# A two-layer decoder trunk on one core: the gating layer norm's scale and shift folded into the mixing's bias step, the rotation of queries and keys on VectorE alone, odd values in two slots

## The chip, the cores and the metric

The kernel runs on 1 core of one Trainium2 chip. The metric is device time in microseconds (us) of one execution. Three runs of the kernel before gave 1886.30, 1886.41 and 1890.41 us; the median is 1886.41.

## The reference

The input is x, 1 x 512 x 1024 in float32. Two layers are computed, each as x + 1/2 SwiGLU(RMSNorm(x)), then x + Mixer(RMSNorm(x)), then x + 1/2 SwiGLU(RMSNorm(x)), with a hidden width of 2816; a last RMSNorm follows. The change touches the two mixers. Cut to what it touches:

```python
def layer_norm(x, g, b):
    mu = mean(x); var = mean((x - mu) ** 2)
    return (x - mu) * rsqrt(var + NORM_EPS) * g + b

def chunked_spatial_gating(z, ln_g, ln_b, w_s, b_s):      # even layer, z = gelu(h @ w)
    u, v = z[..., :512], z[..., 512:]
    v = layer_norm(v as (4 chunks of 128 tokens, 8 groups, 64 channels), ln_g, ln_b)
    w = lower triangle of w_s                             # (8 groups, 128, 128)
    mixed = einsum('gts,nsgd->ntgd', w, v) + b_s          # one bias per group and t
    return u * mixed

def apply_partial_rope(x, cos, sin):                      # on every q and k
    x1, x2, rest = x[..., :8], x[..., 8:16], x[..., 16:]
    return concat([x1 * cos - x2 * sin, x1 * sin + x2 * cos, rest])

def diff_attention(q, k, v, lam, subln_g, lambda_init):   # odd layer, 8 heads, two q/k maps each
    p = softmax(causal(q k^T / 8))                        # for either map
    o = (p[0] - lam * p[1]) @ v                           # v: 128 wide
    return rms_norm(o, subln_g) * (1 - lambda_init)
```

The even mixer concatenates 8 heads of causal attention with the gating's output; both mixers end with an output projection.

## The kernel before, in words

**Arithmetic.** x lies transposed, as 8 tiles of 128 channels x 512 tokens. Every product is made of three matmuls on halves: a float32 matrix is split into a rounded upper half (a copy on ScalarE, called ACT) and the rest (a subtraction on VectorE, called DVE), and `mm3` (L167 to L170) sums hi x hi, hi x lo and lo x hi in PSUM. So each chunk of weights of 128 x 1024 elements costs a copy (L120) and a subtraction (L121), whichever stage it is for. The tiles of the stream are `w_raw`, `w_hi` and `w_lo`.

**Order.** The work of all stages is one list of slots, `Stream` (L69 to L151). A slot has one or two chunks of weights and a function that issues its matmuls. In the mixers `run` (L125 to L140) first issues the splits of this slot's chunks and of the next slot's, then `step`, then the slot's matmuls. `st.later(n, fn)` puts `fn` into the step n slots on, and `st.mids` into the next one. So attention is woven between projections: what a head needs is issued some slots after its queries and keys, ahead of that slot's matmuls. Each engine works its own queue in order; a scheduler fixes that order when the program is built, near the order of the code, and lets some instructions whose inputs come sooner pass others. The chunks come by DMA over the queue of SyncE (SP).

**Even mixer (L782 to L936).** Slots: four chunks for the gate's second half v (`eg`, bank `pv`), four for its first half u (`eu`, bank `pu`), four for the attention's values (`ev`, `pv`), eight for queries and keys of four pairs of heads (`eqk`, `pq`), then the output projection (`eo`). The gate goes through Gelu on ACT into tiles `gv`. `center` (L825) subtracts the group means (`ln_m`) and sums squares (`ln_s`), one slot on for two token tiles and two slots on for the others. `finish_gate` (L836), three slots on, takes the reciprocal root (L191 to L202), multiplies by it on DVE (L840), by the scale on GpSimd (called POOL, L842) and adds the shift on POOL (L843); one slot later `split_gate` (L846) makes the halves `gh` (ACT, L333) and `gl` (DVE, L334). `mix_group` (L866), one for each pair of groups, in the second to fifth slot of `ev` and `eqk`, multiplies by the triangular weights `wsh`, `wsl`, adds the bias `bs` out of PSUM (L880), multiplies by u and splits. Scale and shift are two arrays of 128 x 512 (the same in every partition), loaded at the mixer's begin.

**Queries and keys.** `rotated` (L632) takes a projection out of PSUM. A shuffle on DVE swaps the channels of a pair into `sw` (L638), `q = pq * cos` is on DVE (L639), `sw = sw * sin` (L640) and `q = q + sw` (L641) are on POOL. In the next step the queries or keys are split: ACT copies (L653, keys L661) and DVE subtractions (L654, L662). This runs 24 times: 8 in the even mixer, 16 in the odd one.

**Attention.** For a head, `scores` gives four score products into banks `s`, the masked rows with their maxima (L688, DVE, tiles `e`), and exponentials (ACT, L690). `transposed` turns them through PE (`pt`) and splits them into `ph` (ACT, L711) and `pl` (DVE, L715); the last quarter, `pw`, isn't split. `attend` multiplies with the values into bank `o`. In the even mixer POOL scales the rows (L912), and the result is split by ACT and by DVE (L924, tile `ml`). The steps come EV = (3, 5, 6) slots after the keys. In the odd mixer DVE and POOL combine the two maps (L974 POOL, L976 DVE), and the result is normed over its 128 channels; the steps come OD = (3, 4, 6, 7, 9, 10) slots on.

**Odd mixer (L939 to L1045).** For each pair of heads there are five slots: queries, keys, queries, keys, and one slot of values (`values`, L1011) with two chunks. It makes 96 matmuls of 256 columns: for each of four token tiles eight k-tiles, three matmuls each.

**Room.** There are 8 banks of PSUM, one tag for all; tiles `w_raw`, `w_hi`, `w_lo` share 14 buffers, `e` has 3 and small temporaries have 7.

## Time and profile before

| What | Value |
| --- | --- |
| Median of three runs | 1886.41 us (1886.30 to 1890.41) |
| The profiled execution | 1890.68 us, of which the span from its first to its last instruction is 1888.9 us |
| Mean granted clock of TensorE | 0.986 |
| Busy share of the span | PE 97%, weight loads 88%, DVE 72%, ACT 46%, POOL 22% |
| HBM read and written | 237.40 MB and 2.10 MB, 127 GB/s over the span |
| Even mixer, odd mixer | about 366 to 566 us and 1270 to 1512 us of the span |

PE is TensorE, SP is SyncE. Times in the rows are microseconds unless marked ns. A matmul's duration includes its passage through a pipeline, so matmuls that follow each other overlap, and the distance of two starts is what each of them costs. "Busy" of an engine leaves out the time in which it waits. The granted clock is a share of 2.4 GHz.

### The profile page before, as it was taken

How to read it: one execution, taken by the hardware profiler on the slowest of the kernel's cores; microseconds unless marked ns; L12 is line 12 of the kernel's file. 1: busy time of each engine (PE TensorE's matmuls, PEld its weight loads, DVE VectorE, ACT ScalarE, POOL GpSimd, SP SyncE). 2: the span in 40 equal slices, each digit the busy share in tenths (PEclk: the TensorE clock that was granted, in tenths of full speed). 3: DMA queues.
4: the chain of work that ended last, by engine and by line, in shares of the span. 5: the costliest groups of instructions: out<-in, count | busy, mean ns of one | idle time of the engine just before them, and what ended most of it. 6: DMA issues, size and time to landing. Idle time of an engine off the chain costs nothing.

```text
span 1888.9 us, 29622 instructions
## 1 busy us (share of the span) xinstructions
PE 1834.6 (97%) x11612; PEld 1663.2 (88%) x11612; DVE 1359.1 (72%) x1949; ACT 875.4 (46%) x1302; POOL 415.0 (22%) x369
## 2 busy tenths in 40 slices
PE   7999999999898999999999999999899989999997
PEld 6989989878787989989899998988788779899896
DVE  8857748766758857748976685787798788578484
ACT  6524525433655524525554352544555455345252
POOL 1111011542522111010310111143433221110113
PEclk8999999999998999999999999999999999999999
DMA  7656656422334656656565565542232346566561
GB/s 201 176 141 154 168 122 168 129 66 69 90 97 94 177 141 152 168 124 156 134 152 154 129 178 135 149 135 67 90 90 90 95 95 169 144 157 163 124 160 45
DMA packets 197468, 247.74 MB, mean 131 GB/s; under 512 B 14272, under 2 KB 166480, under 8 KB 197328
## 3 DMA queue, kind: packets, MB, share of 16 engines
q1 hardware_dynamic: 153200, 202.81, 34.6%
q0 software_dynamic: 43552, 41.98, 15.1%
q8 instruction: 91, 1.49, 0.3%
q10 hardware_dynamic: 576, 1.05, 0.1%
q14 instruction: 49, 0.40, 0.1%
HBM read 237.40 MB, written 2.10 MB: 127 GB/s over the span
## 4 chain that ended last, share of the span: by engine, by line
PE 82%; DVE 7%; POOL 4%; ACT 3%; issue 2%; DMA 1%; SPq 0%; DVEq 0%; POOLq 0%; ACTq 0%
PE py L168 10%; PE py L170 10%; PE py L169 9%; PE pA L424 8%; PE pA L425 8%; PE pA L426 8%; PE pD L426 4%; PE pD L425 4%; PE pD L424 4%; PE pB L426 2%; PE pB L425 2%; PE pB L424 2%; POOL q L641 1%; DVE w_lo L121 1%; ACT e L690 1%
## 5 line engine op out<-in xcount | busy, mean ns | idle before, releaser
L120 ACT ACTIVATE w_hi<-w_raw 128x1024 fp32r<-128x1024 f32 (+1 forms) x450 | 467.8, 1042 | 619.7 <-PE py L169 210.9
L121 DVE TENSOR_TENSOR w_lo<-w_raw,w_hi 128x1024 fp32r<-128x1024 f32 (+1 forms) x450 | 558.5, 1242 | 178.6 <-ACT w_hi L120 144.3
L369 POOL DMA_DIRECT2D w_raw<-in_gu x160 | 173.6, 1209 | 985.2 <-DMA w_raw<-in_gu 522.4
L169 PE MATMUL py<-hl,w_hi 128*128 128x512 f32 x704 | 274.2, 389 | 0.0
L170 PE MATMUL py<-hh,w_lo 128*128 128x512 f32 x704 | 273.9, 389 | 0.0
L168 PE MATMUL py<-hh,w_hi 128*128 128x512 f32 x704 | 273.2, 390 | 0.0
L503 DVE SCALAR_TENSOR_TENSOR x<-py,x 128x512 f32<-128x512 f32 x96 | 66.0, 688 | 170.1 <-PE py L170 170.1
L424 PE MATMUL pA<-xh,w_hi 128*128 128x256 f32 x640 | 182.7, 285 | 0.0
L425 PE MATMUL pA<-xl,w_hi 128*128 128x256 f32 x640 | 182.1, 285 | 0.0
L426 PE MATMUL pA<-xh,w_lo 128*128 128x256 f32 x640 | 182.1, 285 | 0.0
L424 PE MATMUL pA<-xt,w_hi 128*128 128x256 f32 x640 | 181.2, 283 | 0.0
L426 PE MATMUL pA<-xt,w_lo 128*128 128x256 f32 x640 | 181.1, 283 | 0.0
L425 PE MATMUL pA<-xt,w_hi 128*128 128x256 f32 x640 | 181.1, 283 | 0.0
L169 PEld LDWEIGHTS py<-hl,w_hi 128*128 128x128 f32 x704 | 132.2, 188 | 27.6 <-DVE hl L482 0.8
L170 PEld LDWEIGHTS py<-hh,w_lo 128*128 128x128 f32 x704 | 132.2, 188 | 27.5
L168 PEld LDWEIGHTS py<-hh,w_hi 128*128 128x128 f32 x704 | 131.9, 188 | 27.8 <-ACT hh L477 1.2
L424 PEld LDWEIGHTS pA<-xh,w_hi 128*128 128x128 f32 x640 | 123.9, 194 | 1.5 <-ACT v L436 1.4
L425 PEld LDWEIGHTS pA<-xl,w_hi 128*128 128x128 f32 x640 | 123.9, 194 | 0.1
L426 PEld LDWEIGHTS pA<-xh,w_lo 128*128 128x128 f32 x640 | 123.9, 194 | 0.0
L424 PEld LDWEIGHTS pA<-xt,w_hi 128*128 128x128 f32 x640 | 122.9, 192 | 0.2 <-ACT v L436 0.2
L426 PEld LDWEIGHTS pA<-xt,w_lo 128*128 128x128 f32 x640 | 122.9, 192 | 0.0
L425 PEld LDWEIGHTS pA<-xt,w_hi 128*128 128x128 f32 x640 | 122.9, 192 | 0.0
(241 smaller groups left out, 4344.5 us busy)
## 6 DMA issues: line engine op xcount, KB each, us to landing
w_raw<-in_gu SPq DMA_DIRECT2D x402, 256.0 KB, 4.0
w_raw<-in_gu POOLq DMA_DIRECT2D x160, 256.0 KB, 5.3
w_raw<-in_wd SPq DMA_DIRECT2D x128, 256.0 KB, 3.0
w_raw<-in_wd SPq DMA_DIRECT2D x64, 192.0 KB, 2.5
w_raw<-in_oqk SPq DMA_DIRECT2D x16, 512.0 KB, 4.0
w_raw<-in_gu SPq DMA_DIRECT2D x14, 512.0 KB, 4.0
ks<-ks SPq DMA_DIRECT2D x24, 256.0 KB, 3.2
w_raw<-in_eqk SPq DMA_DIRECT2D x8, 512.0 KB, 3.7
```

The costliest lines, as they stand in the source:

```text
L120: nc.scalar.activation(hi, raw, AF.Copy)
L121: nc.vector.tensor_sub(lo, raw, hi.bitcast(F32))
L168: nc.tensor.matmul(o, sh, mh, start=first, stop=False)
L169: nc.tensor.matmul(o, sh, ml, start=False, stop=False)
L170: nc.tensor.matmul(o, sl, mh, start=False, stop=last)
L369: nc.gpsimd.dma_start(dst, src, accum_op=OP.add)
L424: nc.tensor.matmul(o, w[0][:, s], t[0], start=new and p + g == 0, stop=False, **go)
L425: nc.tensor.matmul(o, w[0][:, s], t[1], start=False, stop=False, **go)
L426: nc.tensor.matmul(o, w[1][:, s], t[0], start=False, stop=p == 3, **go)
L503: nc.vector.scalar_tensor_tensor(x[d], py[d], 0.5, x[d], op0=OP.mult, op1=OP.add)
L641: nc.gpsimd.tensor_add(q, q, sw)
L690: nc.scalar.activation(e, e, AF.Exp, bias=nm[:, i:i + 1], scale=-1.0, accum_out=su[:, o + i:o + i + 1])
```

## The change

Three parts:

- **Layer norm.** Scale and shift leave the gate: with G the normed gate, W (scale x G + shift) + bias is scale x (W G) + (shift x row sums of W + bias). The two are constant along the tokens that the mixing sums over, one of each for a channel, and after the mixing a channel is a partition. `biases`, four slots on, sums the rows of W by four matmuls with a tile of ones (banks `prow`) and adds shift x sums to `bs` in eight small operations. `mix_group` uses a multiply-add out of PSUM in place of an add. The POOL operations on `g` are gone, the halves of the gate are issued in `finish_gate`, and the scale and shift are loaded as two columns of four.
- **Rotation.** L640 and L641 are on DVE.
- **Odd values.** One slot with two chunks becomes two slots with one chunk each, both summing into the same two banks; the second one evacuates them. A pair of heads has six slots.

`warm` takes a tile of the temporaries in place of one of its own.

```diff
--- before.py
+++ after.py
@@ -169,7 +169,7 @@
         nc.tensor.matmul(o, sh, ml, start=False, stop=False)
         nc.tensor.matmul(o, sl, mh, start=False, stop=last)
 
-    warm = const.tile([P, 1], F32, name="warm")
+    warm = tmp("warm")[:, :1]
     nc.vector.memset(warm, 0.0)
     nc.scalar.activation(warm, warm, AF.Silu)
 
@@ -637,8 +637,8 @@
         sw, q = tmp("sw"), tmp("q")
         nc.vector.stream_shuffle(sw, pq, SWAP)
         nc.vector.tensor_mul(q, pq, cr)
-        nc.gpsimd.tensor_mul(sw, sw, sr)
-        nc.gpsimd.tensor_add(q, q, sw)
+        nc.vector.tensor_mul(sw, sw, sr)
+        nc.vector.tensor_add(q, q, sw)
         st.mids.append(lambda: place(q))
 
     class Pair:
@@ -801,13 +801,27 @@
                 hi, lo = split(ws, "ws", "r2")
                 wsh.append(hi)
                 wsl.append(lo)
-            ln = act.tile([P, 2, T], F32, name="ln", tag="e", bufs=EB)
-            for n, name in enumerate(("lng", "lnb")):
-                box[name] = ln[:, n]
-                nc.sync.dma_start(box[name], a["ln"][n])
+            ln = sm.tile([P, 2, 4], F32, name="ln", bufs=1)
+            for n in range(2):
+                nc.sync.dma_start(ln[:, n], a["ln"][n, 0:1].rearrange("o (m p) -> p (o m)", p=P))
+            box["ln"] = ln
             bs = act.tile([P, T], F32, name="bs", tag="e", bufs=EB)
             nc.sync.dma_start(bs, a["bs"])
-            box["bs"] = bs.rearrange("p (m t) -> p m t", t=P)
+            box["bs"] = bs = bs.rearrange("p (m t) -> p m t", t=P)
+            one = t2k("r2", "ones", F32R)[:, :P]
+            nc.vector.tensor_copy(one, ones1.to_broadcast([P, P]))
+
+            def biases():
+
+                for c in range(2):
+                    b = bank("prow")
+                    nc.tensor.matmul(b, one, wsh[c], start=True, stop=False)
+                    nc.tensor.matmul(b, one, wsl[c], start=False, stop=True)
+                    for i in range(4):
+                        m, r = 2 * c + i // 2, slice(i % 2 * 64, i % 2 * 64 + 64)
+                        nc.vector.scalar_tensor_tensor(bs[r, m], b[r, i * P:(i + 1) * P], ln[r, 1, m:m + 1],
+                                                       bs[r, m], op0=OP.mult, op1=OP.add)
+            st.later(4, biases)
 
         def by_group(g):
             return g.rearrange("p (g d) -> p g d", d=64)
@@ -839,9 +853,7 @@
                 g = cen[t]
                 nc.vector.tensor_tensor(by_group(g), by_group(g),
                                         rs[:, t, :, None].to_broadcast([P, 8, 64]), op=OP.mult)
-                nc.gpsimd.tensor_mul(g, g, box["lng"])
-                nc.gpsimd.tensor_add(g, g, box["lnb"])
-            st.later(1, lambda: [split_gate(t) for t in range(TT)])
+                split_gate(t)
 
         def split_gate(t):
             gh[t], gl[t] = split(cen[t], "g", "h")
@@ -877,8 +889,10 @@
                 bv = b.rearrange("p (n g t) -> p n g t", n=2, g=2)
                 for h in range(2):
                     r = slice(h * 64, h * 64 + 64)
-                    nc.vector.tensor_tensor(mixv[r, 2 * nn:2 * nn + 2], bv[r, :, h],
-                                            box["bs"][r, m:m + 1, :].to_broadcast([64, 2, P]), op=OP.add)
+                    nc.vector.scalar_tensor_tensor(mixv[r, 2 * nn:2 * nn + 2], bv[r, :, h],
+                                                   box["ln"][r, 0, m:m + 1],
+                                                   box["bs"][r, m:m + 1, :].to_broadcast([64, 2, P]),
+                                                   op0=OP.mult, op1=OP.add)
             nc.vector.tensor_mul(mix, mix, u[m])
             if m < 2:
                 mh[4 + m], ml[4 + m] = split(mix, "m", "h")
@@ -1009,15 +1023,27 @@
                 st.later(n, fn)
 
         def values(p):
-            def fn(wa, wb):
-                b = [bank("pv"), bank("pv")]
-                for t in range(TT):
-                    r = slice(t * P, (t + 1) * P)
-                    for k in range(KT):
-                        w = (wa, wb)[k // 4]
-                        s = slice((k % 4) * 256, (k % 4 + 1) * 256)
-                        mm3(b[t // 2][:, (t % 2) * 256:(t % 2 + 1) * 256], norm.hi[k][:, r], norm.lo[k][:, r],
-                            w[0][:, s], w[1][:, s], k == 0, k == KT - 1)
+            b = []
+
+            def half(n):
+                def fn(w):
+                    if n == 0:
+                        b.extend(bank("pv") for _ in range(2))
+                    for t in range(TT):
+                        r = slice(t * P, (t + 1) * P)
+                        o = b[t // 2][:, (t % 2) * 256:(t % 2 + 1) * 256]
+                        for k in range(4 * n, 4 * n + 4):
+                            s = slice((k % 4) * 256, (k % 4 + 1) * 256)
+                            go = {"skip_group_check": True}
+                            nc.tensor.matmul(o, norm.hi[k][:, r], w[0][:, s], start=k == 0 and t % 2 == 0,
+                                             stop=False, **go)
+                            nc.tensor.matmul(o, norm.hi[k][:, r], w[1][:, s], start=False, stop=False, **go)
+                            nc.tensor.matmul(o, norm.lo[k][:, r], w[0][:, s], start=False, stop=k == KT - 1, **go)
+                    if n == 1:
+                        evac()
+                return fn
+
+            def evac():
                 halves = [t2k("h", "v", F32R).rearrange("p (n c) -> p n c", n=2) for _ in range(3)]
                 vh = [halves[t][:, 0] for t in range(TT - 1)]
                 vl = [halves[t][:, 1] for t in range(TT - 1)]
@@ -1025,7 +1051,8 @@
                 for t in range(TT):
                     evac_value(t, b[t // 2][:, (t % 2) * 256:(t % 2 + 1) * 256], norm.col[:, t:t + 1], vh, vl, vw)
                 box["v", p] = (vh, vl, vw)
-            st.add([chunk(a["ov"][p, 0]), chunk(a["ov"][p, 1])], fn)
+            for n in range(2):
+                st.add([chunk(a["ov"][p, n])], half(n))
 
         for h in range(8):
             pair = Pair()
```

Lines after the edits have other numbers in the changed kernel: L840 is L854 there, L858 is L870, L880 is L892, L910 is L924, L924 is L938, L976 is L990.

**DVE, gate of the even mixer.** The rows are the stretch from the product with the reciprocal root to the first weights' splits after it (`gv` the gate, `gl` its lower halves, `u` the gate's other half, `w_lo` the weights). Before:

```order
L840 TENSOR_TENSOR gv<-gv,ln_rs 128x512 x4
L858 TENSOR_TENSOR u<-pu,R 128x512
L334 TENSOR_TENSOR gl<-gv,gh 128x512
L121 TENSOR_TENSOR w_lo<-w_raw,w_hi 128x1024
L334 TENSOR_TENSOR gl<-gv,gh 128x512 x3
L121 TENSOR_TENSOR w_lo<-w_raw,w_hi 128x1024
L858 TENSOR_TENSOR u<-pu,R 128x512
```

In the changed kernel, in the same place:

```order
L854 TENSOR_TENSOR gv<-gv,ln_rs 128x512 x3
L334 TENSOR_TENSOR gl<-gv,gh 128x512
L854 TENSOR_TENSOR gv<-gv,ln_rs 128x512
L334 TENSOR_TENSOR gl<-gv,gh 128x512
L870 TENSOR_TENSOR u<-pu,R 128x512
L334 TENSOR_TENSOR gl<-gv,gh 128x512
L121 TENSOR_TENSOR w_lo<-w_raw,w_hi 128x1024
L334 TENSOR_TENSOR gl<-gv,gh 128x512
L870 TENSOR_TENSOR u<-pu,R 128x512
L121 TENSOR_TENSOR w_lo<-w_raw,w_hi 128x1024 x5
```

The first weights' split stands behind three gate halves where it stood behind one. In the changed kernel DVE also has these rows ahead of the means of the gate (`bs` the bias, `prow` the row sums):

```order
L202 SCALAR_TENSOR_TENSOR rcol<-rs_3760,rs_3759 128x4
L842 TENSOR_REDUCE ln_m<-gv 128x8
L822 SCALAR_TENSOR_TENSOR bs<-prow,ln,bs 64x128 x7
L121 TENSOR_TENSOR w_lo<-w_raw,w_hi 128x1024
L822 SCALAR_TENSOR_TENSOR bs<-prow,ln,bs 64x128
L843 TENSOR_SCALAR ln_m<-ln_m 128x8
L842 TENSOR_REDUCE ln_m<-gv 128x8
L844 TENSOR_TENSOR gv<-gv,ln_m 128x512
```

Eight operations on `bs` stand at this place, between the first `ln_m` and the following ones; before there were none.

**DVE, attention of the even mixer.** The rows are around the third result of a head (`ml`, which frees its bank) and the probabilities after it (`pl`). Before:

```order
L662 TENSOR_TENSOR ks<-q,ks 64x512 x2
L121 TENSOR_TENSOR w_lo<-w_raw,w_hi 128x1024
L910 RECIPROCAL su<-su 128x4
L121 TENSOR_TENSOR w_lo<-w_raw,w_hi 128x1024
L924 TENSOR_TENSOR ml<-o,mh 64x512
L715 TENSOR_TENSOR pl<-pt,ph 128x512
L715 TENSOR_TENSOR pl<-pt,ph 128x384
```

In the changed kernel:

```order
L662 TENSOR_TENSOR ks<-q,ks 64x512 x2
L924 RECIPROCAL su<-su 128x4
L121 TENSOR_TENSOR w_lo<-w_raw,w_hi 128x1024
L938 TENSOR_TENSOR ml<-o,mh 64x512
L715 TENSOR_TENSOR pl<-pt,ph 128x512
L715 TENSOR_TENSOR pl<-pt,ph 128x384
```

One of the two weights' splits ahead of `ml` is gone from this place.

**DVE, odd mixer.** The rows run from the last combination of two maps (`e`) to the first lower halves of probabilities (`pl`), which the first product with values reads; L638 to L641 are the rotation. Before:

```order
L976 SCALAR_TENSOR_TENSOR e<-e,su_12949 128x512
L638 STREAM_SHUFFLE sw<-pq 128x512
L639 TENSOR_TENSOR q<-pq,rope 128x512
L121 TENSOR_TENSOR w_lo<-w_raw,w_hi 128x1024 x2
L715 TENSOR_TENSOR pl<-pt,ph 128x512
L715 TENSOR_TENSOR pl<-pt,ph 128x384
L715 TENSOR_TENSOR pl<-pt,ph 128x256
L638 STREAM_SHUFFLE sw<-pq 128x512
```

In the changed kernel:

```order
L990 SCALAR_TENSOR_TENSOR e<-e,su_12920 128x512
L654 TENSOR_TENSOR qs<-q,qs 64x512
L639 TENSOR_TENSOR q<-pq,rope 128x512
L640 TENSOR_TENSOR sw<-sw,rope 128x512
L715 TENSOR_TENSOR pl<-pt,ph 128x512
L641 TENSOR_TENSOR q<-q,sw 128x512
L715 TENSOR_TENSOR pl<-pt,ph 128x384
L715 TENSOR_TENSOR pl<-pt,ph 128x256
L662 TENSOR_TENSOR ks<-q,ks 64x512 x2
L638 STREAM_SHUFFLE sw<-pq 128x512
L639 TENSOR_TENSOR q<-pq,rope 128x512
L640 TENSOR_TENSOR sw<-sw,rope 128x512
```

The two weights' splits ahead of `pl` are gone from this place, and the rotation's last two operations stand among its pieces.

## Rows read from the trace of the kernel before

**Rows 1.** Page, part 1 (busy us, share, instructions) and part 4 (chain by engine)

```profile
PE 1834.6 (97%) x11612; PEld 1663.2 (88%) x11612; DVE 1359.1 (72%) x1949; ACT 875.4 (46%) x1302; POOL 415.0 (22%) x369
...
PE 82%; DVE 7%; POOL 4%; ACT 3%; issue 2%; DMA 1%; SPq 0%; DVEq 0%; POOLq 0%; ACTq 0%
```

**Rows 2.** Windows: length, busy PE, PEld, DVE, ACT, POOL; clock, DMA share, GB/s

```profile
478.00:522.00 44.00, 37.24 (x178) 30.83 (x177) 33.49 (x78) 29.40 (x73) 20.05 (x23) 0.92 0.29 84
485.00:491.00 6.00, 2.76 (x10) 1.67 (x10) 4.16 (x13) 2.88 (x9) 2.96 (x3) 0.97 0.00 0
1270.00:1512.00 242.00, 232.71 (x1346) 203.54 (x1345) 194.01 (x443) 123.29 (x269) 86.27 (x81) 0.99 0.29 87
1336.00:1348.00 12.00, 5.42 (x24) 4.69 (x23) 11.94 (x16) 5.12 (x9) 6.19 (x5) 0.72 0.49 160
```

**Rows 3.** PE timeline, even mixer: start, duration (us), engine, line, operation, out<-in, shape

```profile
388.31 0.39 PE L170 MATMUL pu<-xh,w_lo 128*128 128x512 f32 x1
388.54 0.39 PE L168 MATMUL pu<-xh,w_hi 128*128 128x512 f32 x1
...
412.77 0.63 PE L170 MATMUL pv<-w_hi,xl 128*128 128x512 f32 x1
413.20 0.63 PE L168 MATMUL pv<-w_hi,xh 128*128 128x512 f32 x1
```

**Rows 4.** Waits of PE, 366 to 566 us: for whom; total us, times, longest

```profile
PE pv L169 <- DVE w_lo L121: 3.1, 2, 2.3
PE s L681 <- DVE ml L924: 3.0, 1, 3.0
```

**Rows 5.** ACT timeline, even mixer; in brackets idle before and who ended it

```profile
416.54 0.63 ACT L333 ACTIVATE gh<-gv 128x512 fp32r<-128x512 f32 x1 [2.75 <-POOL gv L843]
```

**Rows 6.** DVE timeline, even mixer, layer norm and attention

```profile
402.15 4.69 DVE L840 TENSOR_TENSOR gv<-gv,ln_rs 128x512 f32<-128x512 f32 x4
...
408.47 2.28 DVE L121 TENSOR_TENSOR w_lo<-w_raw,w_hi 128x1024 fp32r<-128x1024 f32 x1
...
515.43 1.59 DVE L121 TENSOR_TENSOR w_lo<-w_raw,w_hi 128x1024 fp32r<-128x1024 f32 x1 [1.03 <-ACT w_hi L120]
```

**Rows 7.** Waits of PE, 1262 to 1524 us

```profile
PE o L169 <- DVE pl L715: 6.6, 1, 6.6
```

**Rows 8.** DVE and POOL timelines, odd mixer, ahead of the first P V product

```profile
1338.43 0.67 DVE L639 TENSOR_TENSOR q<-pq,rope 128x512 f32<-128x512 f32 x1
1339.02 4.14 DVE L121 TENSOR_TENSOR w_lo<-w_raw,w_hi 128x1024 fp32r<-128x1024 f32 x2
...
1338.61 1.26 POOL L640 TENSOR_TENSOR sw<-sw,rope 128x512 f32<-128x512 f32 x1 [1.80 <-DVE sw L638]
1339.96 2.12 POOL L641 TENSOR_TENSOR q<-q,sw 128x512 f32<-128x512 f32 x1
```

**Rows 9.** Groups by line and form: busy us, mean ns | idle before, releaser

```profile
L641 POOL TENSOR_TENSOR q<-q,sw 128x512 f32<-128x512 f32 x24 | 37.0, 1542 | 1.6
L640 POOL TENSOR_TENSOR sw<-sw,rope 128x512 f32<-128x512 f32 x24 | 32.5, 1354 | 86.7 <-DVE sw L638 86.6
...
L639 DVE TENSOR_TENSOR q<-pq,rope 128x512 f32<-128x512 f32 x24 | 16.3, 681 | 4.4 <-POOL rope L625 4.2
...
L843 POOL TENSOR_TENSOR gv<-gv,ln 128x512 f32<-128x512 f32 x4 | 6.7, 1692 | 0.2
```

**Rows 10.** One line's view: L121 in 1288 to 1480 us, min/median/max ns

```profile
L121 DVE TENSOR_TENSOR w_lo<-w_raw,w_hi x24: 1184/1225/2280, 1300.9 to 1474.7; 128x1024 fp32r<-128x1024 f32 x24
```

**Rows 11.** Windows of two pairs of heads, odd mixer (columns as rows 2)

```profile
1349.50:1396.80 47.30, 47.23 (x291) 42.16 (x290) 39.09 (x98) 24.64 (x59) 17.48 (x17) 1.00 0.27 78
1396.80:1445.80 49.00, 47.47 (x292) 42.18 (x291) 43.98 (x104) 28.28 (x65) 17.54 (x18) 1.00 0.30 93
```

**Rows 12.** Groups by line and form, DVE: busy us, mean ns

```profile
L688 DVE CUSTOM_DVE_ANT_0 e<-s,mask 128x128 f32<-128x128 f32 x24 | 6.8, 282 | 0.5 <-PE s L682 0.5
```

**Rows 13.** DMA issues: KB each, us from issue to landing

```profile
sg<-in_subg SPq DMA_DIRECT2D x1, 0.5 KB, 5.5
```

## The prediction

> **What bounds the kernel now.** I read the page's shares first, then busy time by stage, then who PE waited for, then the timelines of the stages with waits. The page has PE busy for 97% of the span, and the chain that ended last runs over PE for 82% [rows 1]. So only time in which PE idles, or runs at the lower of its two clock levels, can be had back. The stage table shows where that is in the parts that the change touches: in the attention of the even mixer PE is busy 37.24 of 44.00 us at a mean granted clock of 0.92, and in one 12 us piece of the odd mixer 5.42 us at 0.72, while the odd mixer as a whole has 232.71 of 242.00 [rows 2]. Everything else of the two mixers is packed: matmuls of 512 columns follow each other every 0.23 us, and every 0.43 us where the clock is at 1.2 GHz instead of 2.4 [rows 3].
>
> Three places lose time, and each hangs on in-order engines behind GpSimd:
>
> - Even mixer, layer norm: PE waits 3.1 us in two pieces (2.3 and 0.8) for split halves of the values' weights [rows 4]. ACT stood 2.75 us before the last half of the gate because of L843 on POOL, with the weights' copy queued behind it on ACT [rows 5]. After the first piece eight matmuls ran at the lower clock, 8 x (0.43 - 0.23) = 1.6 us [rows 3]. Some 5 us in all.
> - Even mixer, attention: 44.00 - 37.24 = 6.8 us idle, and (1 - 0.92) x 44 = 3.5 us through the clock; 10 us [rows 2]. The longest piece, 3.0 us, is a score matmul waiting for L924 on DVE to free a bank [rows 4]. L924 stood behind a weights' split that itself idled 1.03 us for ACT and then took 1.59 [rows 6]. The six microseconds from 485 hold another 6.00 - 2.76 = 3.2 us of idle PE [rows 2].
> - Odd mixer: 6.6 us before the first P V product [rows 7]. The lower halves of the probabilities (L715) stood behind two weights' splits that took 4.14 us while POOL added a rotation [rows 8]. With the lower clock after it some 8 us.
>
> **The rotation (24 times).** Off POOL: L640 and L641, 1354 and 1542 ns in the mean. Onto DVE: two operations of 128x512 like L639, 681 ns [rows 9], of which the engine's next instruction overlaps a part (it starts 0.59 after L639 in [rows 8]); I take 0.62. In the odd mixer that is 16 x 2 x 0.62 = 20 us of DVE, 5.0 per pair of heads. Against it: DVE no longer runs beside these POOL operations. A split of 128x1024 takes 1225 ns in the median and up to 2280 [rows 10]; two took 4.14 instead of 2.45 [rows 8], 1.7 us for one rotation. From below the relief is nothing (a rotation that meets no two-input operation), from above 1.7 a rotation; I take 0.7, as most rotations meet one short operation: 16 x 0.7 = 11 us. So DVE gains about 9 us of work in the odd mixer, 194 to 203 of 242 us. Its busiest pair of heads has 43.98 of 49.00, the one before 39.09 of 47.30 [rows 11]; with 5.0 - 4 x 0.7 = 2.2 more they stay under the period of PE. The way from shuffle to rotated tile shortens from 0.7 (a shuffle taken like L639) + 1.35 + 1.54 = 3.6 us with a change of engine to 4 x 0.65 = 2.6 on one, and is no longer behind POOL's softmax scaling (L912, L974).
>
> The Trainium skill (SBUF — State Buffer, Who interferes with whom) says that the port pair of VectorE and GpSimd is an exclusive lock, and that a VectorE operation with two SBUF inputs waits until a GpSimd operation that reads SBUF is done. By that rule a split that meets L640 or L641 is late by up to the whole of it, and the 4.14 us against 2.45 agree in part [rows 8]: 1.7 us late under 3.4 us of POOL work. With the whole of it the relief would be nearer the upper bound, and the odd mixer's DVE would not gain work at all.
>
> What that is worth on PE. Even attention: the order shows one split less ahead of L924, so of its 3.0 us I keep 1.5 and drop the clock loss behind it (1.6); the copies of keys (ACT, behind L641) come about 1 us sooner by the shorter way, which takes half of the 3.2 us from 485, 1.6, and with them part of the rest of the clock loss, 1.2. Together 1.5 + 1.6 + 1.6 + 1.2 = 5.9 of 10, taken as 6.0. Bounds: nothing, and all 10.
>
> **Odd values in two slots.** The matmuls are the same 96 of 256 columns per pair of heads; one slot of 96 x 0.115 = 11 us becomes two of 5.5, and a pair takes six slots, not five. Each weight chunk is split one slot ahead of its own use, so the two splits no longer stand together: in the new order L715 comes before any of them. The first stall goes, 8 us. What is late next: the second head of each pair had the long value slot between its transposes and its P V product, now one query slot of 24 x 0.23 = 5.5 us. In that slot DVE has two halves of keys and the first L715 (0.7 each, taken like L639), a rotation (2.6) and a split (1.2), 5.9 us, of which some starts a slot ahead. I put 0.5 us a pair on it, 2 us for four pairs; from below nothing, from above a whole split and a lower clock each time, 4 x (1.2 + 1.6) = 11. Net gain 6.0; bounds +8 and -3.
>
> **Layer norm folded.** Gone: eight POOL operations of 1.7 us [rows 9] and the wait of ACT for them. Added on PE: four matmuls of 512 columns, 4 x 0.23 = 0.9 us, all of it on the path, since PE is packed there. Added on DVE: eight operations of 64x128 out of PSUM; the nearest row is L688 at 128x128, 282 ns [rows 12], so 8 x 0.28 = 2.3 us, and they stand in front of the means, waiting about 1 us for those matmuls. That is a chain of 3.4 us more before the reciprocal root; behind it four products and three halves run without POOL, 4 x 0.62 + 3 x 0.62 + 0.62 + 1.2 = 6.2 us to the first split instead of 8.6 (402.15 to 408.47 + 2.28 = 410.75 on DVE [rows 6]). So the first split is 1 us later, PE itself 0.9 later: the first wait and its clock loss stay, the second (0.8) goes. 0.9 - 0.8 = about 0. Bounds: a gain of 4 (no wait left), a loss of 4 (1 us more on each of the first three slots and a longer lower clock). The multiply-add that replaces the plain add out of PSUM is one instruction for one. The two 256 KB loads become 1024 elements of 4 bytes at the start of the program; the nearest row, 128 such elements, landed after 5.5 us among other loads [rows 13]. Nothing reads them before 385 us and the chunk behind them is split some 12 us after its issue, so nothing, with 1 us as upper bound. The table of ones costs DVE one short copy while it idles; `warm` and the freed tile cost nothing.
>
> **Sum.** -6.0 - 6.0 + 0 = -12.0 us against the profiled execution's 1890.7, so 1878.7. That execution is the slow end of the runs shown (median 1886.4, 4.3 less); against the median 1874.4, rounded 1874.5.
>
> **Rivals.**
> - *DVE becomes the bound of the odd mixer.* The busiest pair's 5.0 us of DVE idle is time it must wait for ACT, and it does not shrink. With 5.0 us more work and no relief that pair takes 54 instead of 49, and so do two more of the four: 3 x 5 = 15 us, against a gain of 6 in the even mixer: 1886.4 + 9 = 1895.5. It decides from the point where relief is under half the added time in pairs 2 and 3. For it: 43.98 of 49.00 [rows 11]. Against it: 39.09 in the pair before, and the value slots, where DVE was least busy, now take a score step more. Chance 0.11. The Trainium skill (Perfetto Trace Analysis, Optimizing Scalar/DVE Operations) says that work of a saturated VectorE may well be moved off, to GpSimd even; this change goes the other way, and the rule's result would be this rival. Its next sentence, that such moves between those two may not help, agrees with the two splits that took 4.14 us beside POOL [rows 8].
> - *The waits only move.* The layer norm costs 1, the even attention saves 3 (ACT's exponentials stand in the way as before), and the odd slots give back 6 of 8: -4 us, 1882.5. For it: on all three places PE's wait ends on in-order queues with ACT in them. Chance 0.19.
> - *All three places clear*: 5 + 10 + 8 less 0.9, some 22 us: 1864.5. Against it: the ACT copies stay where they were. Chance 0.10.
> - That the change does not do what it says is excluded by the order: L640 and L641 stand on DVE, POOL has no operation on `gv` left but the squares.
>
> **How the numbers follow.** The forecast has 0.60, between 1868 and 1880. Under 0.3% (5.7 us) a measurement of this kernel can't tell from no change. Faster: 0.58 of the forecast, 0.10 of the clearing, 0.02 of the moved waits: 0.70. Slower: 0.09 of the DVE rival. Same: the rest, 0.21. The range reaches from 1866 to 1888: it leaves out most of the clearing below and the DVE rival above.
>
> **What would show it.** Right: L640 and L641 as DVE at about 0.68, splits near 1.23 throughout, no wait of 6 us before `o`, one wait for `w_lo` near 408 us instead of two, `prow` four times at 0.23, DVE of the odd mixer at 200 to 205 us. Wrong: a wait of PE for L715 of over 1 us in every pair of heads, or DVE at 95% in 1300 to 1480 us; or a first wait near 408 us of 4 us and more.

## The result, and the profile after

The changed kernel took 1876.78 us (median of 4 runs, 1874.70 to 1876.98) against 1886.88 us for the kernel before (4 runs). The ratio is 0.9937, 95% interval 0.9923 to 0.9951: 0.63% faster, 11.9 us, between 9.2 and 14.5; the two medians lie 10.1 us apart, which is inside that interval. The forecast was 12 us. The sum came out; two of its three terms did not stand where the prediction put them.

The profiled execution took 1876.65 us with a span of 1874.9. Part 1 and part 4 of its page, which answer to [rows 1]:

```profile
PE 1830.6 (98%) x11616; PEld 1662.5 (89%) x11616; DVE 1371.7 (73%) x2006; ACT 875.1 (47%) x1302; POOL 337.4 (18%) x313
...
PE 87%; DVE 8%; issue 1%; ACT 1%; DMA 1%; POOL 0%; SPq 0%; DVEq 0%; POOLq 0%; ACTq 0%
```

POOL has 77.6 us less to do and is off the chain that ended last, where it had 4%. DVE has only 12.6 us more, though the rotation's 48 operations of about 0.7 us (35 us) and the eight on the bias (3 us) came to it.

The stages are read from the starts of PE's first matmuls of each kind in the timeline: the even mixer's sums (`pc`), its mixing (`mixp`), the next stage (`pg`), the odd mixer's projections (`pq`) and again `pg`. "Gate" is from `pc` to `mixp`, "attention" from there to `pg`; the same table serves for the experiments.

| Kernel | Gate | Attention | Odd mixer | Median us, ratio to before (95% interval) |
| --- | --- | --- | --- | --- |
| before | 56.73 | 150.72 | 247.28 | 1886.88 |
| changed | 57.65 | 141.64 | 243.73 | 1876.78, 0.9937 (0.9923 to 0.9951) |
| e1 fold alone | 54.88 | 151.32 | 247.17 | 1889.90, 1.0004 (0.9995 to 1.0013) |
| e2 rotation alone | 56.74 | 141.63 | 240.94 | 1873.15, 0.9915 (0.9901 to 0.9928) |
| e3 two slots alone | 56.74 | 149.15 | 252.87 | 1894.11, 1.0032 (1.0019 to 1.0044) |
| e4 sums a slot sooner | 54.90 | 141.60 | 244.65 | 1876.17, 0.9932 (0.9920 to 0.9945) |
| e5 changed, one slot | 57.50 | 141.67 | 241.92 | 1874.15, 0.9928 (0.9916 to 0.9940) |
| e6 row a step later | 57.55 | 141.47 | 240.58 | 1873.21, 0.9922 (0.9909 to 0.9936) |
| e7 as e5, bias sums later | 51.88 | 141.46 | 240.91 | 1868.69, 0.9901 (0.9887 to 0.9914) |
| e8 as e7, second split later | 51.85 | 141.64 | 242.23 | 1868.58, 0.9904 (0.9890 to 0.9917) |
| e9 changed, rotation on POOL | 56.51 | 151.33 | 252.98 | 1895.29, 1.0044 (1.0030 to 1.0059) |
| e10 half the rotation on DVE | 56.73 | 148.42 | 247.00 | 1885.44, 0.9990 (0.9980 to 0.9999) |
| e11 e2 and idle POOL work | 56.75 | 145.36 | 254.25 | 1891.48, 1.0018 (1.0009 to 1.0028) |
| e12 e6 and bias sums later | 51.86 | 141.57 | 242.06 | 1868.91, 0.9904 (0.9890 to 0.9919) |

Between the two profiles gate and attention changed by +0.9 and -9.1 and the odd mixer by -3.6, together -11.7; the rest of the 14.0 us between the spans lies in stages that the change does not touch. Kernels of e1 to e4, of e5 to e8 and of e9 to e12 shared their runs of before (medians 1888.07, 1887.49 and 1887.41).

Windows of the changed kernel (columns as in [rows 2]): the attention's piece that was 44.00 us there, and the odd mixer.

```profile
478.00:513.00 35.00, 34.23 (x185) 29.20 (x183) 34.26 (x79) 26.72 (x66) 15.02 (x16) 1.00 0.32 90
...
1264.00:1507.00 243.00, 232.46 (x1344) 203.79 (x1342) 205.31 (x488) 126.15 (x278) 40.56 (x49) 0.99 0.28 85
```

The first piece shrank by 9 us: PE idles 0.8 us in place of 6.8, at the full clock in place of 0.92. DVE now is busy for 34.26 of 35.00 us there; it is nearly full, and the only wait of PE in this piece, 0.7 us, is one for DVE (`pq` for `q`, below).

Waits of PE in the changed kernel, first from 366 to 570 us (answers to [rows 4]), then from 1253 to 1515 us ([rows 7]); the waits for `pg` and `py` are those at the seams to the next stage, which the kernel before has too.

```profile
PE pg L168 <- ACT w_hi L120: 4.9, 1, 4.9
PE pv L169 <- DVE w_lo L121: 1.7, 1, 1.7
PE pv L168 <- ACT w_hi L120: 1.3, 1, 1.3
...
PE pq L168 <- DVE q L639: 0.7, 1, 0.7
PE s L681 <- DVE ml L938: 0.2, 1, 0.2
...
PE pg L168 <- ACT w_hi L120: 5.4, 1, 5.4
PE pr L322 <- DVE ocol L202: 3.6, 2, 3.3
PE py L170 <- DVE w_lo L121: 2.0, 2, 1.5
...
PE o L169 <- DVE pl L715: 0.2, 1, 0.2
```

The score matmul's 3.0 us and the 6.6 us before the P V product are gone (0.2 each). A wait that was 1.1 us is now 3.3: the norm's row (`pr`, L322) for its reciprocal root (`ocol`). The gate has one wait for lower halves in place of two, and one of 1.3 us for upper halves where there were two of at most 0.3. In the kernel before, in the view of [rows 7]:

```profile
PE pr L322 <- DVE ocol L202: 1.1, 1, 1.1
```

The new wait in DVE's timeline, steps of the reciprocal root (L191 to L202) among the other head's scores and a rotation:

```profile
1352.26 0.15 DVE L191 TENSOR_SCALAR rs<-pc 128x4 f32<-128x4 f32 x1
...
1354.88 0.17 DVE L197 TENSOR_SCALAR rs<-rs 128x4 f32<-128x4 f32 x1
1354.95 1.22 DVE L121 TENSOR_TENSOR w_lo<-w_raw,w_hi 128x1024 fp32r<-128x1024 f32 x1
1356.09 0.16 DVE L198 TENSOR_TENSOR rs<-rs,rs 128x4 f32<-128x4 f32 x1
...
1356.17 0.72 DVE L638 STREAM_SHUFFLE sw<-pq 128x512 f32<-128x512 f32 x1
...
1357.52 0.69 DVE L640 TENSOR_TENSOR sw<-sw,rope 128x512 f32<-128x512 f32 x1
1358.12 0.16 DVE L201 TENSOR_TENSOR rs<-rs,rs 128x4 f32<-128x4 f32 x1
1358.24 0.69 DVE L641 TENSOR_TENSOR q<-q,sw 128x512 f32<-128x512 f32 x1
1358.85 0.15 DVE L202 SCALAR_TENSOR_TENSOR ocol<-rs,rs 128x4 f32<-128x4 f32 x1
```

Ten operations of 0.15 to 0.17 us take 6.7 us from the first start to the last end. In the gate, where nothing stands between them, the same ten (on 128x32) took from 403.33 to 405.52, 2.2 us. PE meanwhile idled 3.3 us and then ran at the lower of its two clock levels for a while (mean granted clock 0.58 from 1359 to 1363 us): the ten transposes after it took 1.9 us, those of the next head 1.0.

That a reciprocal root stands among other work is not new. In the kernel before six of the eight did, and took 4.3 to 6.8 us. What is new is how soon PE asks for the result. From the sums (`pc`) to the row (`pr`) of the second head of a pair, the wait for the row taken off, PE took 8.9 to 9.9 us in the kernel before and takes 7.7 to 7.9 now (first three pairs of heads). The first such head in the kernel before, then in the changed one:

```profile
1377.78 0.95 PE L993 MATMUL pc<-ones,sq 128*128 128x1 f32 x8
1386.71 0.62 PE L322 MATMUL pr<-ident,ocol 128*128 128x128 f32 x4
```

```profile
1347.90 0.95 PE L1007 MATMUL pc<-ones,sq 128*128 128x1 f32 x8
1359.06 0.65 PE L322 MATMUL pr<-ident,ocol 128*128 128x128 f32 x4 [3.34 <-DVE ocol L202]
```

The splits of two pairs of heads (the view of [rows 10], 1277 to 1470 us):

```profile
L121 DVE TENSOR_TENSOR w_lo<-w_raw,w_hi x25: 1208/1220/1226, 1291.3 to 1461.6; 128x1024 fp32r<-128x1024 f32 x25
```

The longest was 2280 ns and is 1226; none is stretched any more.

### The profile page after: what moved, and what is told of

Read it like the earlier page. It is cut to its first block, busy times and chain, and to the rows that moved or that the text cites. A ratio compares the mean times of both kernels' runs of the same rounds, so it can differ in the third digit from the quotient of the medians.

```text
span 1874.9 us, 29596 instructions
## 1 busy us (share of the span) xinstructions
PE 1830.6 (98%) x11616; PEld 1662.5 (89%) x11616; DVE 1371.7 (73%) x2006; ACT 875.1 (47%) x1302; POOL 337.4 (18%) x313
## 4 chain that ended last, share of the span: by engine, by line
PE 87%; DVE 8%; issue 1%; ACT 1%; DMA 1%; POOL 0%; SPq 0%; DVEq 0%; POOLq 0%; ACTq 0%
PE py L168 10%; PE py L170 10%; PE py L169 10%; PE pA L424 8%; PE pA L426 8%; PE pA L425 8%; PE pD L426 4%; PE pD L425 4%; PE pD L424 4%; PE pB L424 2%; PE pB L426 2%; PE pB L425 2%; PE pq L168 1%; PE pq L170 1%; PE pq L169 1%; DVE w_lo L121 1%
## 5 line engine op out<-in xcount | busy, mean ns | idle before, releaser
L121 DVE TENSOR_TENSOR w_lo<-w_raw,w_hi 128x1024 fp32r<-128x1024 f32 (+1 forms) x450 | 549.7, 1222 | 172.5 <-ACT w_hi L120 135.7
```

The source lines that it names most:

```text
L121: nc.vector.tensor_sub(lo, raw, hi.bitcast(F32))
```

## Experiments

**Each part alone.** e1 has only the fold (`biases`, `mix_group`, `finish_gate`), with the change of `warm`; e2 has only the rotation; e3 only the two slots:

```diff
-        nc.gpsimd.tensor_mul(sw, sw, sr)
-        nc.gpsimd.tensor_add(q, q, sw)
+        nc.vector.tensor_mul(sw, sw, sr)
+        nc.vector.tensor_add(q, q, sw)
...
-            st.add([chunk(a["ov"][p, 0]), chunk(a["ov"][p, 1])], fn)
+            for n in range(2):
+                st.add([chunk(a["ov"][p, n])], half(n))
```

> The kernel before with the layer norm part alone (and the small tile that makes room for it). Theory (each part keeps its own price): the four row-sum matmuls cost PE 0.9 us, the wait at the first value matmuls stays about as long as it is, so the even mixer is 1 us longer and the odd mixer unchanged: 0 to +2 us against the kernel before. Rival (the fold, through another order on DVE and a freer GpSimd, is what shortened the even mixer's attention by 9 us): 6 to 9 us faster.

> The kernel before with the rotation on VectorE alone. Theory: this is what cleared the even mixer's attention, so that mixer is 8 to 10 us shorter; in the odd mixer the wait of 6.6 us for the lower halves of the probabilities stays at 4 us or more, since two weights' splits still stand ahead of them: 7 to 11 us faster in all. Rival (the attention became shorter through the layer norm's fold or the order that came with it): the even mixer within 3 us of before, in all 0 to 4 us faster.

> The kernel before with the odd values in two slots alone. Theory: the wait of 6.6 us and its clock loss go, 8 us, and the new wait of 3.3 us for the norm's column does not come, since the reciprocal root is not interleaved with a rotation on VectorE: 7 to 9 us faster, the even mixer unchanged. Rival (the new wait comes from the slots' new lengths, whoever rotates): a wait of 3 us or more for the column here too, 2 to 5 us faster.

e1: no change that can be measured. The gate's length is 1.9 us shorter in this one profile, which the last section takes up; the attention is as before, so the rival fell.

e2: 0.85% faster, 16 us (14.9 between the medians), more than the whole change: its slowest run took 1873.50 us, the fastest of the changed kernel 1874.70. The attention's 9.1 us are all the rotation's. The odd mixer also became 6.3 us shorter, for which the theory left hardly anything: 7 to 11 us in all, 8 to 10 of them in the even mixer. Waits of PE in its odd mixer:

```profile
PE o L169 <- DVE pl L715: 2.7, 1, 2.7
PE py L170 <- DVE w_lo L121: 0.8, 1, 0.8
```

The wait that the two slots were thought necessary for fell from 6.6 to 2.7 us by the rotation alone, where the theory kept 4 us or more. The two weights' splits still stand ahead of `pl`, but take 1.21 us each. From PE's product with the upper halves to that with the lower it is 4.17 us in place of 6.97, so `pl` comes 2.8 us sooner; the other 1.1 us are ten transposes that PE now does in that gap. The lower clock behind it went: over the 12 us from the upper halves' product on it is 1.00, against 0.72 in [rows 2].

```profile
1325.00:1337.00 12.00, 9.11 (x63) 8.02 (x62) 11.94 (x17) 5.66 (x10) 1.30 (x2) 1.00 0.44 147
```

e3: 0.32% slower, where 7 to 9 us of gain were expected. Waits of PE in its odd mixer:

```profile
PE pr L322 <- DVE ocol L202: 4.8, 4, 2.8
PE py L170 <- DVE w_lo L121: 2.8, 2, 1.5
PE pq L168 <- DVE v L737: 2.4, 1, 2.4
PE o L168 <- ACT ph L711: 1.2, 1, 1.2
PE o L726 <- ACT pw L711: 0.6, 1, 0.6
PE o L169 <- DVE pl L715: 0.4, 1, 0.4
```

The 6.6 us are gone here too, as predicted, but others came. The wait for the column comes without a rotation on DVE, so it belongs to the slots, as the rival said (its longest is 2.8 us, the rival had 3). The rival's price failed too: it had 2 to 5 us of gain, and the odd mixer is 5.6 us longer than before.

**Leaving one part out.** e5 puts `values` back into one slot, e9 the rotation back on POOL.

> The changed kernel with the odd values back in one slot. Theory (the two slots cost time, and more than they give, because a pair of heads now has six steps and the norm's reciprocal root meets the other head's scores): the odd mixer is 3 us shorter than in the changed kernel and no wait for the norm's column is over 0.5 us; 15 to 17 us faster than the kernel before. Rival (beside the rotation on VectorE the two slots pay, and what the rotation alone gave is used up by the fold): 8 to 11 us faster, a wait of 5 us or more for the lower halves of the probabilities.

> The changed kernel with the rotation's product and sum back on GpSimd, so the fold and the two value slots alone. Theory (the rotation carries the whole gain): attention of the even mixer back at 149 to 151 us, odd mixer at 250 us or more, 1888 to 1896 us, that is 0 to 8 us slower than the kernel before. Rival (the parts overlap, and fold and two slots keep a part of the gain once they stand together): 3 us or more faster than the kernel before.

e5: odd mixer 1.8 us shorter than in the changed kernel (3 expected), no wait for the column over 0.5; 0.72% faster than before, 13.6 us, a little short of the 15 expected but beyond the rival's 11. Its runs (1873.15 to 1874.73) lie below those of the changed kernel but for a hair, so what the two slots cost there is small, 2.6 us between the medians. e9: 8 us slower than the kernel before, as its theory said; without the rotation on DVE the other two parts only cost. The largest waits of its odd mixer repeat those of e3:

```profile
PE pr L322 <- DVE ocol L202: 4.9, 4, 3.0
PE pq L168 <- DVE v L737: 2.4, 1, 2.4
```

**Where the two slots lose.** A pair of heads now has six slots, and a step n slots on comes earlier in time and meets other steps. With OD = (3, 4, 6, 7, 9, 10) and six slots a pair, the sums (9) fall into the step of another head's first scores (3), and the row (10) into that of its second scores (4). With five slots the sums fell into the step of another head's second scores; the sixth slot changes which steps meet and how much work PE has between sums and row. e4 moves the sums a step earlier, e6 the row a step later (for six heads of eight):

```diff
-    OD = (3, 4, 6, 7, 9, 10)
+    OD = (3, 4, 6, 7, 8, 10)
...
-                st.later(n, fn)
+                st.later(n + (fn is r and h < 6), fn)
```

> The changed kernel with the odd norm's sums and reciprocal root one slot sooner (step 8 in place of 9). Theory (the reciprocal root's ten small operations lie between large ones on VectorE and only need a slot more): the wait of 3.3 us for the column and the lower clock behind it go, 4 to 5 us faster than the changed kernel, 14 to 16 us faster than the kernel before. Rival (VectorE has no room in that stretch, and whoever comes later waits for it): another wait of 2 us or more takes its place, within 2 us of the changed kernel.

> The changed kernel with the norm's row one step later (11 in place of 10) for the first six odd heads; the sums and the reciprocal root stay at step 9. Theory (it is the place of these steps among six slots: the row is asked for one short slot after a reciprocal root that stands between the other head's scores): the wait of 3.3 us for the column goes and nothing of 1.5 us takes its place, 3 to 5 us faster than the changed kernel, 13 to 16 us faster than before. Rival (VectorE's work in that stretch is what is late, whatever reads it): a new wait of 2 us or more, within 2 us of the changed kernel.

e4: the wait for the column is gone and three others stand in its place (2.0, 1.2 and 1.0 us; the 1.5 us for `w_lo` the changed kernel has too); the time is that of the changed kernel, and the odd mixer is 0.9 us longer. The rival held. Its waits of PE, 1254 to 1500 us:

```profile
PE pq L168 <- DVE q L639: 2.0, 1, 2.0
PE py L170 <- DVE w_lo L121: 1.5, 1, 1.5
PE s L681 <- DVE o L1015: 1.2, 1, 1.2
PE py L168 <- DVE pl L715: 1.0, 1, 1.0
```

e6: odd mixer 240.58, 3.2 us shorter than in the changed kernel, and nothing of 1.5 us in its place between 1300 and 1480 us:

```profile
PE o L169 <- DVE pl L715: 1.4, 3, 0.7
PE py L168 <- DVE pl L715: 0.8, 1, 0.8
PE o L726 <- ACT pw L711: 0.2, 1, 0.2
```

The medians agree: 1873.21 us, with all runs below those of the changed kernel. So the two slots' cost was the place of one step, and how soon PE asks for the row decides. But with it mended they give no more than one slot: 240.58 against 240.94 in e2.

**The bias sums.** e7 takes e5 and issues the row sums and the eight bias operations at step 9; e8 adds to e7 that the second chunk of a slot with two is split after the step; e12 joins e6 and e7.

```diff
-            st.later(4, biases)
+            st.later(9, biases)
...
-                    if i + 1 < len(self.slots):
-                        self.split_to(self.slots[i + 1][1])
+                    self.split_to(self.slots[i + 1][0] + 1 if i + 1 < len(self.slots) else 0)
                     self.step()
+                    self.split_to(self.slots[i + 1][1] if i + 1 < len(self.slots) else 0)
```

> As e5, with the row sums and their eight bias operations five slots later (step 9 in place of 4), behind the layer norm's chain. Theory (the eight operations and their wait for the row sums are 3.4 us of the chain ahead of the reciprocal root): the reciprocal root starts some 3 us sooner, the first wait at the value matmuls (1.3 for the upper and 1.7 for the lower halves in the changed kernel) falls below 1 us, and the kernel is 2 to 4 us faster than e5. Rival (the wait hangs on the last column sums, which wait for GpSimd's squares and so for the products of PE): the wait stays within 0.5 us of what it is, same as e5.

> As e7, with the second chunk of a slot that has two (the odd values) split after the step in place of before it, so that one weights' split less stands ahead of the first lower halves of probabilities. Theory (the 2.7 us that the rotation alone left there are such splits): that wait falls by 1.2 us or more, 1 to 3 us faster than e7. Rival (the copies on ScalarE or the softmax ahead of them set the end): the wait stays over 2 us, within 1 us of e7.

> All three parts of the change, with the norm's row one step later (as e6) and the row sums five slots later (as e7). Theory (both waits have their own cause, so both gains add up): gate at 52 us, odd mixer at 240.6 us, 1867 to 1869 us, as fast as e7 or up to 1.5 us faster. Rival (a mixer that starts sooner runs into another wait): 2 us or more slower than e7.

e7: 0.99% faster than before, 18.7 us, and its interval lies apart from that of the changed kernel. Counted from the stage's first sums, the reciprocal root ends 34.0 us on, in place of 38.2 in the changed kernel, and of the gate's waits this is left (366 to 561 us):

```profile
PE pv L169 <- DVE w_lo L121: 0.3, 1, 0.3
```

The gate lost 5.6 us against e5, more than the 2 to 4 expected, because the lower clock went with the waits (0.85 in e5 and 1.00 in e7, 405 to 428 us). e8: the wait for `pl` fell by 0.4 us only (2.3) and small ones appeared elsewhere; same as e7. Its rival named the right time but not the cause. The halves do come sooner without the second split: from PE's product with the upper halves to that with the lower it is 3.04 us in place of 4.20. But PE has three transposes to do in that gap and not ten, so less of it is filled. e12: same as e7 too, with an odd mixer of 242.06 us and not 240.6. e7 is the simplest of the three and beats both kernels.

e7 is also e2 with the fold and late bias sums, and it is 4.5 us faster than e2 (medians 1868.69 and 1873.15, runs apart), with a gate 4.9 us shorter. So the fold pays once its sums are out of the way; alone and as placed in the change, it gave nothing.

**Why the rotation pays.** e10 leaves the sum (L641) on POOL. e11 is e2 with two more operations on POOL behind each rotation, whose result nothing reads:

```diff
-        nc.gpsimd.tensor_mul(sw, sw, sr)
+        nc.vector.tensor_mul(sw, sw, sr)
...
-        nc.gpsimd.tensor_add(q, q, sw)
+        nc.vector.tensor_add(q, q, sw); nc.gpsimd.tensor_mul(sw, cr, sr); nc.gpsimd.tensor_add(sw, sw, cr)
```

> The kernel before with only the rotation's product (L640) on VectorE; the sum (L641) stays on GpSimd. Theory (what counts is that GpSimd's operations no longer lengthen VectorE's and the rotated tile comes sooner, each in proportion): between the two, the even mixer's attention at 144 to 148 us, 4 to 9 us faster than before. Rival (it is the change of engines that costs, once or twice alike): attention at 149 us or more, within 3 us of before.

> The kernel of e2 (rotation on VectorE alone) with two operations of the same size added on GpSimd behind each rotation, on a tile that nothing reads any more; GpSimd has the work of before again, the rotation's way stays on VectorE. Theory A (the gain came from the shorter way of the rotated tile): attention at 143 us or less, within 4 us of e2. Theory B (it came from VectorE and GpSimd no longer working side by side, or from GpSimd's queue ahead of the softmax scaling): splits of 1.6 us and more in the trace again, attention at 147 us or more, 6 us or more slower than e2.

e10: 2 us faster than before, attention 2.3 us shorter, a quarter of what the whole rotation gave; the time is the rival's, the attention lies between the two. e11: 18 us slower than e2.

In the attention 3.7 of the 9.1 us are lost again, with POOL busier there than before (58.60 us against 52.35). 2.5 of them are waits of PE's transposes for the softmax scaling on POOL (L912), which stood behind the added work. The waits for DVE that the kernel before had did not come back. In e10, where the sum is still on POOL and the rotated tile still waits for it, the score matmul's wait stayed. From 424 to 570 us in e11, then from 423 to 572 us in e10:

```profile
PE pt L702 <- POOL e L912: 2.5, 2, 1.7
...
PE s L681 <- DVE ml L924: 0.2, 1, 0.2
```

```profile
PE s L681 <- DVE ml L924: 2.7, 1, 2.7
```

So the 5.4 us that stayed gained hang on the rotation's way and not on POOL's load. Whether it is the sooner tile, or the order on DVE that the scheduler builds from it, no run separates.

In the odd mixer 13.3 us are lost, more than the rotation had given. Windows of e2 and of e11 over the odd mixer:

```profile
1263.00:1504.00 241.00, 231.74 (x1347) 202.04 (x1345) 207.59 (x488) 126.53 (x278) 41.08 (x50) 1.00 0.28 86
```

```profile
1268.00:1522.00 254.00, 238.04 (x1346) 206.79 (x1344) 222.01 (x488) 127.09 (x278) 89.89 (x82) 0.97 0.27 82
```

DVE has the same 488 instructions and is busy 14.4 us longer, 0.90 us for each of 16 rotations' worth of POOL work (two operations, 3.1 us). That is what POOL's operations cost beside DVE here. The groups show where: the halves of queries and keys right behind a rotation rose from 687 and 684 ns to 928 and 903, and some steps of the reciprocal root from 0.16 to 0.35 us, while the rotation's L639, which reads only one of its inputs from SBUF, stayed at 681. L654 over the same windows, e2 first:

```profile
L654 DVE TENSOR_TENSOR qs<-q,qs 64x512 fp32r<-64x512 f32 x16 | 11.0, 687 | 0.5
```

```profile
L654 DVE TENSOR_TENSOR qs<-q,qs 64x512 fp32r<-64x512 f32 x16 | 14.9, 928 | 0.5
```

The Trainium skill (SBUF — State Buffer, Who interferes with whom) says that a VectorE operation with two SBUF inputs contends with a GpSimd operation that reads SBUF; the 222.01 us against 207.59 and the rise of L654, which has two such inputs, agree. The shares hold for this arrangement: the added operations run behind a rotation and not inside it.

## Why the prediction was right in sum, and where it was wrong

- **Rotation, even attention: -6.0 forecast, -9.1 measured.** The mechanism held, step by step: the score matmul's wait went (3.0 to 0.2), the waits from 485 us went, and so did the clock loss. It was near the upper bound of 10, because no wait over 0.7 us stayed; the halves that the sum kept of 3.0 and 3.2 us were the mis-sized terms. That the tile comes sooner and that the order has one split less could not be told apart (e11).
- **Rotation on DVE's time.** Forecast +9 us in the odd mixer, 194 to 203. e2 alone has 207.59 against 199.38 for the kernel before over the same work (1274 to 1521 us), +8.2. Relief was taken at 0.7 a rotation; with the 0.62 us that the prediction took for an added operation, +8.2 means 0.73, and POOL work put behind the rotations cost 0.90 (e11). The rival in which DVE becomes the bound did not come: DVE was busy 86% of 1300 to 1480 us in the changed kernel, and 205.31 us in its odd mixer, just above the 200 to 205 that was to be the sign.
- **Odd values in two slots: -6.0 forecast; wrong.** The odd mixer did lose 3.6 us, but the rotation alone gave 6.3 and the slots took some back: 2.8 us against e2, 1.8 against e5, 5.6 if they stand alone. Two steps failed. The first stall was put down to the two splits standing together, and its whole 8 us to parting them; with the splits left together and only POOL's rotation out of the way it fell to 2.7 us and the lower clock went (e2). And "what is late next" was sought at the second head's P V product, at 0.5 us a pair; that place waited 0.2 us. The norm's row, one step behind a reciprocal root of ten small operations, was not looked at: with six slots PE asks for it one to two us sooner, which cost 3.3 us and a lower clock behind it (e6 removes them).
- **Layer norm: 0 forecast, +0.9 in the profile, nothing that can be measured alone (e1).** Its chain was a little too short. Counted from the stage's first sums (368.07 us in the kernel before, 367.32 in the changed one), the reciprocal root's first product came 4.2 us later (forecast 3.4) and the first split ended 1.6 us later (forecast 1); the eight bias operations took 0.36 us each, not 0.28. The row sums took 4 x 0.23 us, as forecast. The second wait went, but 1.3 us for upper halves came, so PE waited 3.0 us there in all, where it had 3.6. The clock loss, which the prediction kept as it was, differs by execution (last section). What the prediction did not ask is whether that chain had to stand there; e7 says no, and it was worth 5.6 us.
- **The rest.** The small loads of scale and shift landed after 5.3 us and delayed nothing that can be seen: the even mixer's first sums came at 367.32 us (368.07 in the kernel before). Some additions of the prediction are rounded by 0.1 or 0.2 us, which changes nothing.

That the two wrong terms nearly cancelled is luck: 3.1 us too little for the attention, 2.4 too much for the odd mixer.

## What to carry to other kernels

A change of several parts is to be forecast part by part and tried part by part: here one part gave 16 us, one nothing where it was placed, and one took some back. When steps are scheduled by slots, adding a slot moves every step of the chain against the others, so look for the longest chain of small operations whose reader stands one step behind it, and count the time that the reader leaves it. Work whose result is wanted late, like the bias sums, belongs behind a critical chain on its in-order queue, even where it is short.

## What the hardware showed that was not expected

The same waits cost a different time from one execution to another. Windows of 23 us around the gate's wait, the changed kernel first, then e1, whose gate is built alike:

```profile
405.00:428.00 23.00, 19.97 (x80) 15.88 (x79) 15.67 (x24) 9.52 (x12) 0.00 (x0) 0.85 0.28 94
```

```profile
405.00:428.00 23.00, 19.97 (x93) 16.13 (x92) 15.94 (x22) 10.16 (x13) 0.00 (x0) 1.00 0.30 92
```

PE was busy for 19.97 us in both and waited 1.3 and 1.7 us in both. In one the granted clock fell behind the wait (0.85, and 80 matmuls done), in the other it stayed (1.00, and 93). The gates differ by 2.8 us; e5 and e6 are like the first, e4 is like the second, and e9 lies between (0.93, gate 56.51). The attention of e3, which e3 does not touch, is 1.6 us shorter than before in the one profile. The profile of a single execution cannot place a few microseconds where PE's wait is of that length.
